# A transformer layer on one core: the merge's elementwise work is taken off the pool engine, and weights are split by whole chunks

## The chip, the cores and the metric

The program runs on one core of a Trainium2 chip. The time is the device time of one execution in microseconds (us). The engines have separate instruction streams and meet at semaphores: PE multiplies matrices (with its weight load, PEld), DVE, ACT and POOL work elementwise, and SP issues most of the loads.

## The reference

One layer for 1024 tokens of width 1024, with 256 context tokens, all in fp32:

```
h   = rmsnorm(x, norm1)*(1+sc1) + sh1                  # in-projection, attention and mLSTM read this
x   = x + g1 * ((sig(g_mla)*attention + sig(g_ml)*mlstm) @ w_out)
h2  = rmsnorm(x, norm2)*(1+sc2) + sh2
aff = softmax(h2 @ w_router)                           # 16 experts
gate, idx = top_k(aff.T, 128)                          # each expert takes its 128 best tokens
y_e = ((silu(xs @ w_gate_e) * (xs @ w_up_e)) @ w_down_e) * gate,   xs = h2[idx_e]
x   = x + g2 * scatter_add(y);   out = rmsnorm(x, final_norm)
```

The result is compared at fp32 accuracy. The kernel splits every operand of a large product into a rounded high part (type fp32r) and the rest as a low part, and adds three products: high by high, high by low, low by high. So each weight has a cast (the high part, on ACT) and a subtraction (the low part) before PE can use it.

## The kernel before, in words

The stages follow one another: norm and in-projection (to about 560 us), the mLSTM and the query projection, attention from about 815 us, the merge from 1258 us, the end of the top-k search from 1402 us, the experts from 1434 us to 2010 us, and the final norm. A scheduler has fixed each engine's order when the program was built; each engine then works in that order, and an instruction that waits holds all behind it.

**Attention** works in 32 groups (8 heads by 4 blocks of 256 queries). For each group PE writes scores `s` for all 1280 keys in five tiles of 128x512. `scores` (L1515 to L1539) takes the running maximum `mx` on DVE (L1529, then four of L1532) and folds it into `mm` (L1536). PE transposes `mm` (L1545, in `peak`), DVE reduces again (L1548), and the maximum goes back as a row that is added to the scores by further products, after which ACT takes the exponent (L1584, `exps`). POOL adds the exponents up (L1590). `low` subtracts on DVE (L1599, tiles `tl`), `finish` (L1632 to L1636) multiplies the group's output by its gate and its denominator (`w`, L1630 and L1635) and adds it to the array `xca` that the out-projection reads (L1636).

**The merge** takes eight tiles of 128 tokens. `half` (L1021) makes high and low parts of the out-projection's weight, eight subtractions of 128x1024 at L1024; those in the table `POOL` go to POOL, the others to DVE. `prep` (L1028) does the same for a tile of `xca` (L1032: tile 0 on DVE, tiles 1 to 7 on POOL). `project` multiplies (L983), adds to the residual (L1086, L1087) and takes the norm's factor `rs` with a Newton iteration on DVE (L1094, L154 to L159). `route` transposes the tile, multiplies by the router's weights and takes the softmax (L1130 to L1134). `store_h` writes the normalized tokens to memory: ACT scales by `rs` (L1139), POOL multiplies by norm2's scale (L1143) and adds its shift (L1147). `largest` finds candidates for each expert's 128 best (MAX8 and MATCH_REPLACE8, L940 and L942, and merges of sorted lists with minimum and maximum, L913 and L914). It runs at tiles 4, 5, 6 and 7, with lists of 64, 16, 16 and 16. `top.last` ends the search with the threshold `thr` (L967).

**The experts** come from one stream of chunks of 1 MB, 12 for each expert: 0 to 3 and 4 to 7 for gate and up (tiles `pa`, `pu`), 8 to 11 for down (`py`). `Weights.load` issues a chunk into one of 16 raw buffers (`raw_l`, `xca`, `ha`, `raw_e`, all lent by other stages), `Weights.split` makes `hi` and `lo` of half a chunk, 128x1024, into one of four pairs of buffers (cast L875 on ACT, subtraction L876 on DVE, on POOL for the first three). `products` asks for the split four halves ahead. `pick(e)` marks on POOL which token stands at which place (L1257, eight operations of 128x128), lets PE sum the marks into indices (`aux`, L1190), and gathers the tokens `xg` with an indirect DMA (L1278). It is called two experts ahead, after chunk 5. `turn_x` transposes gathered tokens on PE (L1287) and splits them (`xh`, L1289, and `xl`, L1290); `turn` does the same for the hidden values (`hd`). At an expert's end DVE scales `py` into `y` (L1353) and POOL adds it to memory (L1354).

Of the kernel before, what the change touches and what calls it, by code (L numbers as in the profile page):

```python
# [23 lines left out]
F32 = mybir.dt.float32  # L24
# [35 lines left out]
N_HAP, N_EARLY, N_MID, N_LATE, N_HI = 2, 3, 4, 7, 4  # L60
# [6 lines left out]
POOL = ((4, 0), (6, 0), (2, 1), (6, 1))  # L67
# [8 lines left out]
def body(tc, A, out, dbg=None, upto=99):  # L76
# [669 lines left out]
    with ExitStack() as s6:  # L746
# [17 lines left out]
        moe(tc, A, out, aff, thr, W, h2_d, acc_d, ident, rstd_dve, dump)  # L764
# [5 lines left out]
class Weights:  # L770
# [19 lines left out]
    def ahead(self):  # L790

        self.wout = [self.outputs(2 * m, self.wide(F32)) for m in range(N_HAP)]
        self.rows = [[self.row(self.narrow(), r, o, 512) for o in (0, 512)] for r in (0, 2)]
# [11 lines left out]
    def load(self, upto):  # L805
        while self.loaded < min(upto, 12 * NE):
# [3 lines left out]
            if j in ONCE:  # L810
                t = self.once[j]
                loads = [self.nc.sync.dma_start(t[c], src[:, c, :]) for c in range(self.begun.pop(j, 0), 2)]
            else:
                b = self.buffer(SEQ.index(j) if j < len(SEQ) else j - 2)
                t = b[:, 0], b[:, 1]
# [3 lines left out]
            if self.after is not None:  # L819
# [4 lines left out]
                if j >= N_RAW + 2 or j in (ONCE[0], 14, 15, 16, 17):  # L824
                    self.after = None
# [32 lines left out]
    def halves(self):  # L858
        return [self.hi.tile([P, D], F32R, name=x, bufs=N_HI) for x in ("hi", "lo")]

    def split(self, upto, engine=None):

        while self.cut < min(upto, 24 * NE):
            j, c = divmod(self.cut, 2)
            self.load((SEQ.index(j) if j < len(SEQ) else j) + 1)
            w = self.raw[j][c]
            if self.cut < 24 * NE - 8:
                hi, lo = self.halves()
            else:
                both = self.buffer(self.cut - 12 * NE + 6, F32R)  # L870
                hi, lo = both[:, 0, :], both[:, 1, :]
            self.parts[self.cut] = hi, lo
            if len(w.shape) == 3:
                hi, lo = [t.rearrange("p (c d) -> p c d", d=256) for t in (hi, lo)]
            self.nc.scalar.copy(hi, w)  # L875
            done = (engine or self.nc.vector).tensor_sub(lo, w, hi)  # L876
# [93 lines left out]
class Merge:  # L970
# [50 lines left out]
    def half(self, k, hf, h, l):  # L1021
        w = self.raw[k][:, :, hf * 512:hf * 512 + 512]
        self.nc.scalar.copy(h, w)
        (self.nc.gpsimd if (k, hf) in POOL else self.nc.vector).tensor_sub(l, w, h)  # L1024
# [3 lines left out]
    def prep(self, i, t):  # L1028
# [3 lines left out]
        (self.nc.vector if i == 0 else self.nc.gpsimd).tensor_sub(ml, self.xca[:, :, c], mh)  # L1032
# [19 lines left out]
    def rest(self, aff, thr, pool):  # L1052
# [7 lines left out]
        g1r, a2 = W.rows  # L1060
        t = W.last(N_FIRST + 1)
        t_buf = t[:, 0, :]
        sh2 = W.row(t[:, 1, :], 1, 0, D)

        def project(i):
# [5 lines left out]
            for hf in order:  # L1071
                o = slice(hf * 512, hf * 512 + 512)
                if (i, hf) not in self.ps:
# [5 lines left out]
                    elif i >= 4:  # L1079
# [29 lines left out]
        def largest(i):  # L1109
            n, part = (64, aff[:, 4:8]) if i == 4 else (16, aff[:, 8 - i:10 - i])  # L1110
# [933 lines left out]
```

## Time and profile before

| what | value |
|---|---|
| median of 3 runs | 2041.03 us (2039.46 to 2044.31) |
| the profiled execution | 2041.3 us, span 2039.5 us, granted clock 0.979 |
| PE busy | 1910.6 us, 94% |
| DVE, ACT, POOL busy | 1462.2, 1048.9, 602.0 us |
| attention to merge to experts | 816, 1258, 1434 us |
| last product | 2010.4 us |

The span runs from the first to the last instruction of the profiled execution; its own time is 1.8 us more. PE's busy share says little on its own, since a few per cent of idle time is all that other engines can give back. So the reading goes by stage: in which stretch PE stands still, and for whom.

### The profile page before, as it was taken

The numbers are of one execution on the slowest core, as the hardware profiler recorded it, in microseconds if no ns is written. First come the engines' busy times: TensorE is split into PE (matmuls) and PEld (weight loads), VectorE is DVE, ScalarE is ACT, GpSimd is POOL, SyncE is SP. The second block draws the span as 40 slices with busy tenths as digits, with TensorE's granted clock in tenths as the row PEclk, the third lists the DMA queues.
The fourth block names the chain that finished last, engine by engine and source line by source line (L and its number), as shares of the span: only waits on it lengthen the run. The fifth ranks groups of instructions, "written<-read, shape, count | busy, mean of one in ns | idle before, by whom it ended". The sixth has DMA issues, their size and how long they took to land. (4 is left out here: it accounts for less than half of the span.)

```text
span 2039.5 us, 28755 instructions
## 1 busy us (share of the span) xinstructions
PE 1910.6 (94%) x10458; PEld 1614.1 (79%) x10458; DVE 1462.2 (72%) x2704; ACT 1048.9 (51%) x1677; POOL 602.0 (30%) x527
## 2 busy tenths in 40 slices
PE   7999999999999999899999998985999999999994
PEld 3898888888877878889998987863778778787873
DVE  6454555112477888687877788578899999999997
ACT  5554421123247676434334434321777777777774
POOL 0000000000043040275434446433453634536310
PEclk9999999999999999999999998997999999999997
DMA  7143376222187060323111111636899999999975
GB/s 302 58 149 100 106 248 220 76 93 89 61 279 248 22 221 1 94 71 117 50 47 50 37 53 58 246 133 224 292 375 380 372 381 369 383 382 364 388 240 187
DMA packets 156301, 385.84 MB, mean 189 GB/s; under 512 B 10224, under 2 KB 94784, under 8 KB 137088
## 3 DMA queue, kind: packets, MB, share of 16 engines
q1 hardware_dynamic: 141104, 329.73, 44.9%
q0 software_dynamic: 12752, 45.90, 7.4%
q10 hardware_dynamic: 2304, 8.39, 1.1%
q8 instruction: 82, 1.34, 0.3%
q14 instruction: 59, 0.48, 0.1%
HBM read 327.04 MB, written 56.93 MB: 188 GB/s over the span
## 5 line engine op out<-in xcount | busy, mean ns | idle before, releaser
L86 PE MATMUL mm<-hT,whi 128*128 128x512 f32 (+1 forms) x1392 | 414.8, 381 | 2.6 <-DVE hT L305 2.3
L86 PEld LDWEIGHTS mm<-hT,whi 128*128 128x128 f32 x1392 | 255.1, 189 | 52.0 <-DVE hT L305 2.4
L86 PE MATMUL mm<-hT,wlo 128*128 128x512 f32 (+1 forms) x696 | 262.9, 378 | 0.3 <-DVE wlo L90 0.3
L876 DVE TENSOR_TENSOR lo<-raw_l,hi 128x1024 fp32r<-128x1024 f32 x156 | 188.1, 1235 | 11.2 <-ACT hi L875 8.2
L1257 POOL TENSOR_SCALAR g<-iota,slot 128x128 bf16<-128x128 f32 x120 | 192.4, 1624 | 0.0
L875 ACT CAST hi<-raw_l 128x1024 fp32r<-128x1024 f32 x156 | 163.3, 1053 | 48.2 <-PE pu L1190 33.8
L1190 PE MATMUL py<-hi,hd 128*128 128x512 f32 x480 | 160.8, 399 | 0.0
L86 PEld LDWEIGHTS mm<-hT,wlo 128*128 128x128 f32 x696 | 131.2, 189 | 24.5 <-DVE wlo L90 0.7
L90 DVE TENSOR_TENSOR wlo<-wraw,whi 128x1024 fp32r<-128x1024 f32 x38 | 46.5, 1224 | 142.8 <-ACT whi L89 142.8
L1590 POOL TENSOR_TENSOR es<-es,e 128x512 f32<-128x512 f32 x96 | 126.4, 1317 | 7.0
L1590 POOL TENSOR_TENSOR es<-e 128x512 f32<-128x512 f32 x32 | 41.8, 1305 | 272.4 <-ACT e L1584 272.4
L876 DVE TENSOR_TENSOR lo<-xca,hi 128x1024 fp32r<-128x1024 f32 x96 | 115.3, 1231 | 6.6 <-ACT hi L875 4.8
L1584 ACT ACTIVATE e<-s 128x512 f32<-128x512 f32 x160 | 94.5, 612 | 47.1 <-PE s L1432 47.1
L1354 POOL DMA_INDIRECT acc_d<-y,idx x15 | 34.9, 2328 | 270.4 <-DVE y L1353 270.4
L875 ACT CAST hi<-xca 128x1024 fp32r<-128x1024 f32 x96 | 100.1, 1051 | 27.6 <-PE pu L1190 20.0
L89 ACT CAST whi<-wraw 128x1024 fp32r<-128x1024 f32 x38 | 40.0, 1051 | 128.8 <-PE mm L86 120.4
L1190 PEld LDWEIGHTS py<-hi,hd 128*128 128x128 f32 x480 | 89.7, 188 | 17.9
L1190 PE MATMUL pa<-hi,xh 128*128 128x512 f32 x256 | 102.4, 400 | 0.3 <-ACT xh L1289 0.3
L1190 PE MATMUL pa<-lo,xh 128*128 128x512 f32 x256 | 99.9, 390 | 1.1 <-DVE lo L876 1.1
L1190 PE MATMUL pu<-lo,xh 128*128 128x512 f32 x256 | 99.8, 390 | 0.0
L1190 PE MATMUL pu<-hi,xl 128*128 128x512 f32 x256 | 99.8, 390 | 0.0
L1190 PE MATMUL pa<-hi,xl 128*128 128x512 f32 x256 | 99.7, 390 | 0.0
(509 smaller groups left out, 5088.2 us busy)
## 6 DMA issues: line engine op xcount, KB each, us to landing
raw_l<-in_wgu SPq DMA_DIRECT2D x54, 1024.0 KB
xca<-in_wgu SPq DMA_DIRECT2D x33, 1024.0 KB
raw_l<-in_wd SPq DMA_DIRECT2D x28, 1024.0 KB
raw_e<-in_wgu SPq DMA_DIRECT2D x24, 1024.0 KB
wraw<-in_win SPq DMA_DIRECT2D x38, 512.0 KB
wt<-in_wmod_b SPq DMA_DIRECT2D x32, 512.0 KB
ha<-in_wgu SPq DMA_DIRECT2D x16, 1024.0 KB
xca<-in_wd SPq DMA_DIRECT2D x15, 1024.0 KB
```

Source lines behind the costliest of these rows:

```text
L86: return TE.matmul(o, l, r, start=start, stop=stop, skip_group_check=True)
L89: S.copy(hi, raw)
L90: V.tensor_sub(lo, raw, hi)
L875: self.nc.scalar.copy(hi, w)
L876: done = (engine or self.nc.vector).tensor_sub(lo, w, hi)
L1190: return TE.matmul(o, l, r, start=start, stop=stop, skip_group_check=True)
L1257: G.tensor_scalar(oh[:, o, :], iota, slot[:, o, e:e + 1], None, op0=ALU.is_equal)
L1354: G.indirect_dma_start(out=acc_d, out_offset=bass.IndirectOffsetOnAxis(ap=idx[e][:, :1], axis=0), in_=y, in_offset=None, compute_op=ALU.add)
L1584: S.activation(E[p], ps, AF.Exp)
L1590: G.tensor_add(s, E[0] if p == 1 else s, E[p])
```

## The change

- **Attention.** `finish` no longer adds `w` to `xca`. The addition is kept in a table `ADD` and issued one group later, in `peak2`, behind the last `tl` there. `w` has three buffers for two.
- **Merge.** All subtractions of `half` and `prep` go to DVE. `store_h` only scales by `rs` on ACT and stores; norm2's scale and shift are no longer loaded as rows. `largest` runs at tiles 4, 6 and 7, with lists of 64, 32 and 16.
- **Gathered tokens.** `turn_x` applies norm2's scale and shift after the transposition, where they are a number for each partition: eight operations of 128x128 an expert, on ACT (half of them on DVE for expert 0), from PSUM into a buffer of 128x512 that is then split.
- **Splits.** A cast and a subtraction take a whole chunk, 128x2048, into one of three pairs of whole buffers; `products` asks three chunks ahead. The first is on DVE too. Raw buffers go from 16 to 14, and the loads ahead of the experts from (1, 3, 6, 6, 7, 7, 9, 9) by tile to (1, 3, 4, 4, 5, 5, 7, 7).
- **Picking.** The marks (`mark`) are asked for after chunk 3, and the sums and the gather (`pick`) after chunk 9.
- **Tail.** The last loads and stores of the tokens use contiguous rows of 1024.

```diff
 class Weights / constants
-N_HAP, N_EARLY, N_MID, N_LATE, N_HI = 2, 3, 4, 7, 4
+N_HAP, N_EARLY, N_MID, N_LATE, N_HI = 2, 1, 4, 7, 3
-POOL = ((4, 0), (6, 0), (2, 1), (6, 1))
     def halves(self):
-        return [self.hi.tile([P, D], F32R, name=x, bufs=N_HI) for x in ("hi", "lo")]
+        return [self.hi.tile([P, 2, D], F32R, name=x, bufs=N_HI) for x in ("hi", "lo")]
     def split(self, upto, engine=None):
...
-            self.nc.scalar.copy(hi, w)
-            done = (engine or self.nc.vector).tensor_sub(lo, w, hi)
+            for h, l, w in views:
+                self.nc.scalar.copy(h, w)
+                done = (engine or self.nc.vector).tensor_sub(l, w, h)
 half, prep
-        (self.nc.gpsimd if (k, hf) in POOL else self.nc.vector).tensor_sub(l, w, h)
+        self.nc.vector.tensor_sub(l, w, h)
-        (self.nc.vector if i == 0 else self.nc.gpsimd).tensor_sub(ml, self.xca[:, :, c], mh)
+        self.nc.vector.tensor_sub(ml, self.xca[:, :, c], mh)
 project, largest
-                    elif i >= 4:
+                    elif i in (4, 6, 7):
-            n, part = (64, aff[:, 4:8]) if i == 4 else (16, aff[:, 8 - i:10 - i])
+            n, part = {4: (64, aff[:, 4:8]), 6: (32, aff[:, 2:4]), 7: (16, aff[:, 1:3])}[i]
 store_h
-            if i < 7:
-                S.activation(u, x, AF.Copy, scale=rs)
-            for hf in range(2):
...
-                    G.tensor_mul(u[:, o], u[:, o], a2[hf])
...
-            added = G.tensor_add(u, u, sh2)
+            scaled = S.activation(u, x, AF.Copy, scale=rs)
             nc.scalar.dma_start(self.h2_d[i * P:(i + 1) * P], u)
 rest
-            W.load((1, 3, 6, 6, 7, 7, 9, 9)[i])
+            W.load((1, 3, 4, 4, 5, 5, 7, 7)[i])
-        W.split(N_HI - 1, G)
+        W.split(1)
 moe
         with tc.issue_after(counted.ins):
-            done = W.split(N_HI)
+            done = W.split(2)
         def turn_x(e, q):
...
+            for c in range(4):
+                k, o = 4 * q + c, slice(c * P, (c + 1) * P)
+                sc, sh = bcols[:, 16 + k:17 + k], bcols[:, 8 + k:9 + k]
+                if e == 0 and c % 2:
+                    V.tensor_scalar(t[:, o], tr[:, o], sc, sh, op0=ALU.mult, op1=ALU.add)
+                else:
+                    S.activation(t[:, o], tr[:, o], AF.Identity, scale=sc, bias=sh)
+            hi, lo = [x[:, 4 * q:4 * q + 4, :].rearrange("p a b -> p (a b)") for x in xsT[e]]
+            split(hi, lo, t)
         def products(j, ps, l, start, stop):
-                W.split(2 * j + c + N_HI)
+            W.split(j + N_HI)
+            W.load(N_RAW + j + N_HI + 2 - sum(o < j + N_HI for o in ONCE))
...
-                    if hf == 1 and q == 1 and e + 2 < NE:
-                        pick(e + 2)
+                    if hf == 0 and q == 3 and e + 2 < NE:
+                        mark(e + 2)
...
+                    if q == 1 and e + 2 < NE:
+                        pick(e + 2)
                     if q in (1, 2):
                         turn_x(e + 1, q - 1)
 the tail
-                    nc.sync.dma_start(x[:, a], acc_d[i * P:(i + 1) * P].rearrange("p (c d) -> p c d", d=256))
+                    nc.sync.dma_start(x[:, a], acc_d[i * P:(i + 1) * P])
 attention: peak2, finish
                 for p in PARTS[2:]:
                     low(g - 1, p)
+                if g > 1:
+                    add(g - 2)
...
-            V.tensor_add(xc[h][:, c], xc[h][:, c], w)
+            ADD[g] = xc[h][:, c], w
+            if g >= NG - 2:
+                add(g)
```

Three places of the engines' orders show what moves. In the rows stand the line, the operation, out<-in by the program's names, and the size of the output; line numbers after the change are those of the changed file. The first is DVE in the middle of attention, from one group's gate to the next; before, the addition (L1636) stands ahead of the four maxima (L1532):

```order
L1630 TENSOR_TENSOR w<-s,g_9475 128x256
L1635 TENSOR_TENSOR w<-pv,w 128x256
L1529 TENSOR_REDUCE mx<-s 128x256
L1636 TENSOR_TENSOR xca<-xca,w 128x256
L1532 TENSOR_TENSOR mx<-mx,s 128x512 x4
L1536 TENSOR_TENSOR mm<-mx 128x256
L1599 TENSOR_TENSOR tl<-e,th 128x512
```

With the change:

```order
L1650 TENSOR_TENSOR w<-s,g_9470 128x256
L1655 TENSOR_TENSOR w<-pv,w 128x256
L1547 TENSOR_REDUCE mx<-s 128x256
L1550 TENSOR_TENSOR mx<-mx,s 128x512 x4
L1554 TENSOR_TENSOR mm<-mx 128x256
L1619 TENSOR_TENSOR tl<-e,th 128x512
L1566 TENSOR_REDUCE mq<-sm 128x2
L1619 TENSOR_TENSOR tl<-e,th 128x512
L1579 TENSOR_TENSOR qm_9851<-sm,qm_9851 32x256
L1619 TENSOR_TENSOR tl<-e,th 128x512
L1663 TENSOR_TENSOR xca<-xca,w 128x256
L1454 TENSOR_TENSOR kl_9865<-s,kh_9864 128x512
```

The addition (L1663) now stands behind the third `tl`, and nothing is between the first maximum and the four that follow.

The second is DVE at the end of the top-k search, from the threshold to the first indices. Before, one half-chunk subtraction (L876) stands between the counting (L1235) and the places `slot` (L1250):

```order
L967 TENSOR_REDUCE thr<-bt_13580 16x1
L1211 CAST cst<-g_13609 128x256
L1231 TENSOR_TENSOR mk<-aff,tr 128x8x16
L1232 TENSOR_TENSOR mk<-aff,tr 128x8x16
L1235 TENSOR_REDUCE above<-mk 128x16
L876 TENSOR_TENSOR lo<-ha,hi 128x1024
L1248 SCALAR_TENSOR_TENSOR g_13644<-tr,mk 128x256
L1250 SCALAR_TENSOR_TENSOR slot<-g_13644 128x128
```

With the change:

```order
L971 TENSOR_REDUCE thr<-bt_13501 16x1
L1208 CAST cst<-g_13529 128x256
L1228 TENSOR_TENSOR mk<-aff,tr 128x8x16
L1229 TENSOR_TENSOR mk<-aff,tr 128x8x16
L1232 TENSOR_REDUCE above<-mk 128x16
L880 TENSOR_TENSOR lo<-ha,hi 128x2048
L1245 SCALAR_TENSOR_TENSOR g_13564<-tr,mk 128x256
L880 TENSOR_TENSOR lo<-raw_e,hi 128x2048
L1247 SCALAR_TENSOR_TENSOR slot<-g_13564 128x128
```

Two whole-chunk subtractions stand there now; a third (chunk 0) stands further ahead, between the last MAX8 and the minima of the last merge.

The third is DVE from an expert's last hidden half (`hd`) to its output (`y`). Before, half-chunk subtractions alternate with the small work:

```order
L1290 TENSOR_TENSOR hd<-tr,hd 128x512
L876 TENSOR_TENSOR lo<-ha,hi 128x1024 x2
L1290 TENSOR_TENSOR xl<-tr,xh 128x512
L876 TENSOR_TENSOR lo<-raw_e,hi 128x1024 x2
L1290 TENSOR_TENSOR xl<-tr,xh 128x512
L876 TENSOR_TENSOR lo<-raw_e,hi 128x1024
L1353 SCALAR_TENSOR_TENSOR y<-py_15958,gt,g2row 128x512
```

With the change:

```order
L880 TENSOR_TENSOR lo<-raw_l_15281,hi 128x2048
L880 TENSOR_TENSOR lo<-raw_l_15299,hi 128x2048
L1290 TENSOR_TENSOR hd<-tr,hd 128x512
L1270 COPY ax<-tr 128x5
L1273 SCALAR_TENSOR_TENSOR idx<-ax 128x1
L1274 TENSOR_TENSOR gt<-ax 128x1
L880 TENSOR_TENSOR lo<-raw_l_15322,hi 128x2048
L1275 TENSOR_TENSOR gt<-gt,ax 128x1
L1184 TENSOR_TENSOR xl<-g_15684,xh 128x512
L880 TENSOR_TENSOR lo<-raw_l_15347,hi 128x2048
L1371 SCALAR_TENSOR_TENSOR y<-py_15613,gt,g2row 128x512
```

The last hidden half stands behind the subtractions of chunks 10 and 11, the indices of the pick behind it, and the second half of the gathered tokens behind `y`.

More of the change, by code (lines that the diff above doesn't have):

```diff
@@ L763, in body @@
             return
-        moe(tc, A, out, aff, thr, W, h2_d, acc_d, ident, rstd_dve, dump)
+        moe(tc, A, out, aff, thr, W, h2_d, acc_d, ident, bcols, rstd_dve, dump)
     hap.__exit__(None, None, None)
@@ L792, in ahead @@
         self.wout = [self.outputs(2 * m, self.wide(F32)) for m in range(N_HAP)]
-        self.rows = [[self.row(self.narrow(), r, o, 512) for o in (0, 512)] for r in (0, 2)]
+        self.rows = [self.row(self.narrow(), 0, o, 512) for o in (0, 512)]
     def wide_hi(self, dtype):
@@ L813, in load @@
             else:
-                b = self.buffer(SEQ.index(j) if j < len(SEQ) else j - 2)
-                t = b[:, 0], b[:, 1]
+                t = b = self.buffer(SEQ.index(j) if j < len(SEQ) else j - 2)
                 if len(b.shape) == 4:
@@ L1059, in rest @@
         nc.sync.dma_start(wr, A["wrouter"])
[L1060 to L1063, printed above, removed]
+        g1r = W.rows
+        t_buf = W.last(N_FIRST + 1)[:, 0, :]
         def project(i):
@@ L1182, in rest, with moe, split @@
         self.st.close()
-def moe(tc, A, out, aff, thr, W, h2_d, acc_d, ident, rstd, dump):
+def moe(tc, A, out, aff, thr, W, h2_d, acc_d, ident, bcols, rstd, dump):
     nc = tc.nc
     V, S, G, TE = nc.vector, nc.scalar, nc.gpsimd, nc.tensor
+    def split(hi, lo, raw):
+        S.copy(hi, raw)
+        V.tensor_sub(lo, raw, hi)
     def mm(o, l, r, start, stop):
@@ L1250, in moe, with mark @@
         V.scalar_tensor_tensor(slot, taken[:, :, 0, :], -1.0, taken[:, :, 1, :], op0=ALU.add, op1=ALU.add)
-        gat, idx, xg, xsT, hid = {}, {}, {}, {}, {}
-        def pick(e):
-            oh = W.narrow().bitcast(BF16).rearrange("p (a b) -> p a b", b=P)
+        gat, idx, xg, xsT, marks = {}, {}, {}, {}, {}
+        def mark(e):
+            oh = marks[e] = W.narrow().bitcast(BF16).rearrange("p (a b) -> p a b", b=P)
             for o in range(8):
@@ L1260, in pick @@
                                 slot[:, o:o + 4, e:e + 1].to_broadcast([P, 4, P]), op=ALU.is_equal)
+        def pick(e):
+            oh = marks.pop(e)
             ap = ps7.tile([P, 512], F32, name="tr", bufs=2)
@@ L1317, in act @@
             return h
+        mark(0)
         picked, got, W.after = pick(0)
@@ L1323, in moe @@
         with tc.issue_after(W.after.ins):
+            mark(1)
             pick(1)
@@ L1628, in weigh2 @@
             tr = along(*W[g])
-            w = W[g] = p5.tile([P, 256], F32, name="w", bufs=2)
+            w = W[g] = p5.tile([P, 256], F32, name="w", bufs=3)
             V.tensor_mul(w, tr, G1[g // 2][:, cols(g)])
```

64 lines of the change are left out of this document (36 added, 28 removed).

## The prediction

> **What bounds the kernel now.** I read the busy times by stage first, then PE's waits in each stage, then the timelines of the engines waited for. The window view has for each stretch (start to end, length) the busy us and instructions of PE, PEld, DVE, ACT and POOL, then granted clock, DMA share and GB/s:
>
> ```profile
> 816.00:1225.00 409.00, 388.21 (x2892) 363.00 (x2892) 309.45 (x545) 161.79 (x329) 193.89 (x169) 0.99 0.20 65
> 1258.00:1326.00 68.00, 63.34 (x313) 51.23 (x312) 46.20 (x70) 23.32 (x44) 41.55 (x19) 0.92 0.59 210
> 1326.00:1402.00 76.00, 64.13 (x326) 50.05 (x325) 61.52 (x280) 20.06 (x41) 25.72 (x15) 0.96 0.52 183
> 1402.00:1434.00 32.00, 9.77 (x50) 6.95 (x49) 24.00 (x76) 3.29 (x7) 18.21 (x22) 0.57 0.47 179
> 1470.00:1978.00 508.00, 493.17 (x2351) 404.37 (x2350) 473.81 (x502) 392.56 (x422) 219.66 (x144) 1.00 1.00 367
> ```
>
> PE stands still for 21 us in attention, 17 in the merge, 22 at the end of the search and 15 in the experts. These idle times are the purse; no edit takes products away. I take each part of the change against the stretch that it lies in. The sum is made against the profiled execution, 2041.3 us, which is 0.3 us above the median of the runs.
>
> **Attention.** PE's wait in the stretch 860 to 1225, then the addition over the whole program, then one group's DVE and PE rows:
>
> ```profile
> PE sm L1545 <- DVE mm L1536: 13.8, 25, 1.0
> ...
> L1636 DVE TENSOR_TENSOR xca<-xca,w x32: 419/1398/2603, 855.4 to 1268.2; 128x256 f32<-128x256 f32 x32
> ...
> 1018.73 3.05 DVE L1532 TENSOR_TENSOR mx<-mx,s 128x512 f32<-128x512 f32 x4
> 1021.82 0.61 DVE L1536 TENSOR_TENSOR mm<-mx 128x256 f32<-128x256 f32 x1
> ...
> 1020.22 0.28 PE L1432 MATMUL s<-qp,kpe 128*128 128x256 f32 x1
> 1021.66 0.28 PE L1432 MATMUL pv<-th,vl 128*128 128x256 f32 x1
> 1022.49 0.44 PE L1545 MATMUL sm<-ident,mm 128*128 128x128 f32 x2 [0.55 <-DVE mm L1536]
> ```
>
> The addition takes 0.42 us alone, but 1.40 at the median, and it stands ahead of the four maxima that PE's transposition needs. Without it they start 1.4 us earlier, and another limit takes over: the last score is written at 1020.22 + 0.28 = 1020.50, its maximum takes 0.76 (3.05 for four) and the fold 0.61, so `mm` is there at about 1021.87 for 1022.43. PE is free at about 1021.8. So about 0.45 of each 0.55 us goes: 25 waits give 13.8 x 0.45/0.55 = 11.3, and the three groups before 860 about 1 more. I take **-12**, between -8 (a quarter of it lost to the addition where it lands) and -14 (all of it). The addition now stands ahead of `kl`, `ri` and the next gate. DVE has holes of about 0.5 us there, and POOL's sums are done by then, so at 0.42 it is hidden; beside POOL it would cost up to 1 us in some groups, which is the -8.
>
> **The start of the merge.** PE's first products of the merge, the weight's subtractions on DVE, and the same subtraction where POOL is not in the way:
>
> ```profile
> 1262.76 0.80 PE L983 MATMUL mm<-wl,x 128*128 128x512 f32 x1 [2.81 <-DVE wl L1024]
> 1266.60 0.69 PE L1555 MATMUL mm<-ident,ri 128*128 128x128 f32 x2 [1.34 <-DVE ri L1624]
> 1270.07 0.63 PE L983 MATMUL mm<-wl,x 128*128 128x512 f32 x1
> 1270.49 1.05 PE L983 MATMUL mm<-wh,x 128*128 128x512 f32 x2
> 1272.52 0.39 PE L983 MATMUL mm<-wl,x 128*128 128x512 f32 x1
> 1272.75 0.62 PE L983 MATMUL mm<-wh,x 128*128 128x512 f32 x2
> ...
> L1024 DVE TENSOR_TENSOR wl<-ha,wh 128x1024 fp32r<-128x1024 f32 x2 | 6.7, 3386 | 0.0
> ...
> L876 DVE TENSOR_TENSOR lo<-raw_l,hi 128x1024 fp32r<-128x1024 f32 x156 | 188.1, 1235 | 11.2 <-ACT hi L875 8.2
> ```
>
> A subtraction of this size takes 1.24 us on a free DVE and 3.39 here, where POOL subtracts too. Each is held by 2.1 us, so two on the path return up to 4.2, bounded by the two waits, 2.81 + 1.34 = 4.15. Behind the wait products also start only every 0.42 us (1270.07 to 1270.49) for 0.23 later (1272.52 to 1272.75). From 1262.8 to 1271.8 that is about 17 products, 3.3 us. On the other side four subtractions come to DVE from POOL, 4 x 1.24 = 5 us, of which I put 1.5 in front of products that need them. The sum is -4.15 - 3.3 + 1.5 = **-6**; bounds -8 (nothing in front) and -3 (all 5 in front).
>
> The clock gate in the Trainium skill (TensorE: Matmul & The Clock Gate, Part 1) halves PE's clock after an idle window of about 3.4 us and restores it after a busy one of the same length. By that rule the slow stretch would cost 3.4/2 = 1.7 us, and this part would come to -4.4. The trace shows the slow rate for 9 us, with a second wait in it, so the measurement decides.
>
> **The middle of the merge.** PE's waits from 1258 to 1402, then two groups of DVE instructions (busy us, mean ns of one) in that stretch, and a run of products:
>
> ```profile
> PE tr L1121 <- issue: 6.3, 2, 3.4
> PE so L954 <- DVE bt L914: 2.2, 1, 2.2
> PE so L946 <- DVE rv L154: 1.6, 2, 1.4
> PE tr L1121 <- DVE x L1087: 1.0, 1, 1.0
> ...
> L1087 DVE TENSOR_TENSOR x<-x,raw_l 128x512 f32<-128x512 f32 x8 | 9.4, 1174 | 1.2 <-DMA x<-in_x 1.1
> L1134 DVE TENSOR_SCALAR aff<-aff,mx 128x16 f32<-128x16 f32 x7 | 7.0, 995 | 0.1
> ...
> 1372.29 2.77 PE L983 MATMUL mm<-raw_l,raw_l 128*128 128x512 f32 x6
> ```
>
> L1134 works on 16 numbers a partition and takes 995 ns, where its neighbours of that size take 0.2: it is held while POOL works. L1087 takes 1.17 for 0.68 (the row of 512 columns below). These two groups alone return 7 x 0.8 + 8 x 0.5 = 9.6 us of DVE. PE's waits here are 11.1 us, and the six products in 2.77 us are a slow stretch behind the 3.4 us wait (0.46 each for 0.23); two such stretches add some 3, so about 14 can be won. Part of it stays: the search's waits (L954, L946) depend on sorts that remain at tiles 4, 6 and 7. Against it stand seven `prep` subtractions that come to DVE, 7 x 1.24 = 8.7 us, and for it the search at tile 5 that goes; the last one, below, runs from 1411.66 to 1421.53, 9.9 us with 2.0 of holding, so about 8. These two cancel. I take 14 - 4 = **-10**, between -14 and -4 (the `prep`s on DVE stand ahead of the residual's additions and hold the transpositions by 1.2 us at five or more tiles).
>
> **The end of the search.** From the last tile to the first product of an expert everything is one chain on DVE, with short steps on PE. Its rows, with POOL's work that holds them:
>
> ```profile
> 1401.52 2.40 DVE L914 TENSOR_TENSOR sd<-se 16x64 f32<-16x64 f32 x1
> 1403.85 2.30 DVE L159 SCALAR_TENSOR_TENSOR rs<-rt,ry 128x1 f32<-128x1 f32 x1
> 1408.55 2.39 DVE L1134 TENSOR_SCALAR aff<-aff,mx 128x16 f32<-128x16 f32 x1
> 1411.66 0.21 DVE L940 MAX8 sc<-so 64x8 f32<-64x64 f32 x1
> 1416.82 2.20 DVE L913 TENSOR_TENSOR se<-sd 16x64 f32<-16x64 f32 x1
> 1421.53 0.28 DVE L924 TENSOR_TENSOR bt<-sd,best 16x128 f32<-16x128 f32 x1
> ...
> 1401.50 4.64 POOL L876 TENSOR_TENSOR lo<-ha,hi 128x1024 fp32r<-128x1024 f32 x2 [11.54 <-ACT hi L875]
> ```
>
> Four small operations take 9.3 us for about 0.8, so POOL's leaving returns 8.5, and the two scalings of tile 7 (L1146, 0.7 each) 1.4. Into this chain come three subtractions of a whole chunk. From 1.24 for 1024 columns and 0.68 for 512 (below), 0.56 for each 512, such a one takes about 2.3 on DVE. One stands in the last merge, two behind the counting in place of one of 1.2: 3 x 2.3 - 1.2 = +5.7. The scale and shift of the gathered tokens add about +1.2, four short operations each on ACT and DVE. Together -8.5 - 1.4 + 5.7 + 1.2 = **-3**. If the subtractions fall where DVE waits for PE anyway it is -7; if POOL's remaining casts hold DVE as before, +1.
>
> **The experts.** PE's waits from 1470 to 1990, the outputs' first and last start, eight marks beside busy DVE and beside an idle one, and a subtraction of 512 columns and two casts of 1024:
>
> ```profile
> PE tr L1190 <- POOL g L1257: 13.6, 12, 1.1
> ...
> L1353 DVE SCALAR_TENSOR_TENSOR y<-py,gt,g2row x30: 740/744/747, 1470.4 to 1978.0; 128x512 f32<-128x512 f32 x30
> ...
> 1510.23 13.86 POOL L1257 TENSOR_SCALAR g<-iota,slot 128x128 bf16<-128x128 f32 x8
> 1428.98 4.70 POOL L1257 TENSOR_SCALAR g<-iota,slot 128x128 bf16<-128x128 f32 x8
> ...
> 1521.73 0.68 DVE L1290 TENSOR_TENSOR hd<-tr,hd 128x512 fp32r<-128x512 f32 x1
> ...
> 1407.43 1.98 ACT L875 CAST hi<-ha 128x1024 fp32r<-128x1024 f32 x2
> ```
>
> An expert takes (1978.0 - 0.7 - 1470.4)/14 = 36.2 us. PE waits 1.1 in most of them for the last mark. Moved to the end of chunk 9, `pick` comes some 12 us later, and that wait goes: -13.6. Another takes its place. Chunk 8's end frees the buffer for chunk 11: cast 2.0, subtraction 2.3, and behind both the last `hd`, 0.7, ready 5.1 us after chunk 8 with the handovers. PE reaches the next transpositions, which need its PSUM buffer, after four transpositions, 12 products, the eight short sums and four products: 0.4 + 16 x 0.23 + 0.2 = 4.3. So it waits about 0.8 at 14 handovers: +11. For the last two experts the order puts a subtraction ahead of or behind `y` where PE needs it, +0.8 each. Together -13.6 + 11 + 1.6 = **-1**. Bounds: -8 (half of the handovers hidden, and nothing at the last two) and +8 (a whole 2.3 instead of 0.8 at some six handovers). PE's waits in this stretch name no load, with 16 buffers and 367 GB/s; with 14 an expert's 12 chunks still fit ahead of it, so I cost that at nothing, and two chunks' time, 6 us, is what the stock ahead of PE shrinks by. In the tail the same chain stays, **-0.5** for larger descriptors.
>
> **The sum** is -12 - 6 - 10 - 3 - 1 - 0.5 = -32.5: 2041.3 - 32.5 = **2009 us**.
>
> **Rivals.** *DVE takes POOL's place in the merge.* For it: DVE is busy 61.5 of 76 us before anything is added, and it gets 11 subtractions, 13.6 us. Against it: much of that is time held, 9.6 us in the two groups alone. If a third is won, the start, the middle and the end give -6 for -19: 2041.3 - 12 - 6 - 1.5 = 2022. Chance 0.16. *The scores bound attention.* If the maxima, which follow the scores one by one, leave only 0.1 of the 0.55 to win, attention gives -3 for -12: 2018. Against it stands 1.4 us of addition in front of them. Chance 0.08. *The change finds no idle time to return*, because each wait is replaced by one as long: 2041. Chance 0.03. *Marks too late: slower.* Eight marks take 4.70 us alone and 13.86 beside half-chunk subtractions, 1.73 each, 0.5 more than a subtraction. Beside 2.3 they take 8 x 2.8 = 22. They are asked for after chunk 3, six chunks of 3.03 = 18 us before the sums. If they start only then, PE waits 4 us at 14 experts, +56 and the 0.8 on top: 2041.3 - 31.5 + 56 + 11 = 2077. It decides from 18 us for eight marks. Against it: in POOL's order they stand right behind the gather before, so they can start some 12 chunks ahead. Chance 0.07.
>
> The Trainium skill (SBUF — State Buffer, Who interferes with whom) states that a DVE instruction with two SBUF inputs and a reading GpSimd one exclude each other for a whole instruction. That is the pricing of this last rival; the trace agrees at 1401.52, where 0.2 became 2.40 beside a POOL operation of 2.3.
>
> **How the numbers follow.** My forecast has 0.66. Faster by over 0.2% (4 us, about what a measurement of this kernel can tell) are it and the first two rivals, 0.90; within it 0.03; slower 0.07. The bounds of the terms, taken together, reach from about 1990 to above 2030, and hardly all lie at one end: the range 1995 to 2029 takes in the first two rivals and leaves out the slow one.
>
> **What would show it.** Right: the wait of `sm` for `mm` under 4 us; `wl` and L1134 at 1.2 and 0.2 us; no slow stretch of products in the merge; 1402 to 1434 shorter by about 3; outputs `y` 36.1 apart, with PE waiting at the gathered tokens for `hd`, not for marks. Wrong: marks on PE's waits, a merge as long as before with DVE full, or experts more than 36.6 apart.

## The result and the profile after

The changed kernel takes 2005.79 us (median of 4 runs, 2002.72 to 2007.51) against 2041.2 us: a ratio of 0.9823, with a 95% interval of 0.9806 to 0.9841. That is 35.4 us less; forecast were 32, to 2009. The total was right, most of its terms were not, and the experiments below say why.

I cut both traces at the same instructions: the first transposition of `mm` in attention, the first product of the merge, the softmax of tiles 0 and 7 (its last step), the first product of expert 0, and PE's last product. The lengths between them, in us:

| stretch | before | after | difference | forecast |
|---|---|---|---|---|
| start to attention | 832.4 | 834.5 | +2.1 | 0 |
| attention | 426.2 | 419.8 | -6.4 | -12 |
| merge, to the softmax of tile 0 | 38.5 | 29.4 | -9.1 | -6 |
| merge, to the softmax of tile 7 | 111.5 | 93.4 | -18.1 | -14.3 |
| end of the search, to the first product | 25.4 | 28.5 | +3.0 | +1.3 |
| experts | 576.8 | 573.0 | -3.8 | -1 |
| tail | 28.7 | 26.4 | -2.3 | -0.5 |
| span | 2039.5 | 2004.9 | -34.6 | -32.5 |

(Forecast: two of the four held operations that the prediction counted at the end, L914 and L159, 4.3 us, lie ahead of tile 7's softmax and are counted in the merge here.) The first row lies in stages that the change does not touch and moves between 832.4 and 835.5 in the profiles below. Where a kernel leaves the other stretches alone, attention and the start of the merge repeat to about 1 us either way, the rest to a few tenths. So the runs below are read by stretches, and by medians for the sum.

The window view of the changed kernel, for attention, the merge, the end of the search and the experts (columns as in the prediction):

```profile
816.00:1221.00 405.00, 388.32 (x2895) 360.70 (x2894) 296.67 (x555) 163.29 (x335) 195.43 (x169) 0.99 0.21 65
1254.00:1377.00 123.00, 119.83 (x636) 96.49 (x634) 80.71 (x326) 43.66 (x86) 1.09 (x3) 1.00 0.59 209
1377.00:1405.50 28.50, 9.04 (x53) 6.62 (x53) 20.53 (x79) 6.99 (x9) 10.43 (x19) 0.59 0.64 252
1444.70:1942.80 498.10, 490.26 (x2342) 400.14 (x2342) 456.16 (x333) 399.42 (x364) 248.47 (x142) 1.00 1.03 378
```

The merge is now all but full on PE: 119.8 of 123.0 us at a clock of 1.00, where it was 127.6 busy of 150.0 at 0.93. DVE works 80.7 us in it where it was 113.6 busy, although it got 11 subtractions more and only one search less. In attention 16.7 us of idle time stay. Here are two of PE's waits before, from 860 to 1225, and then its waits in the changed kernel from 800 to 1225, from 1376 to 1408 and from 1443 to 1945. A single wait of 6.6 us ahead of the first maximum (6.0 before) is left out:

```profile
PE sm L1555 <- DVE mq L1548: 0.9, 3, 0.3
PE s L1621 <- DVE kl L1436: 0.2, 1, 0.2
...
PE sm L1573 <- DVE mq L1566: 3.6, 19, 0.5
PE sm L1563 <- DVE mm L1554: 3.4, 6, 1.2
PE s L1641 <- DVE kl L1454: 1.8, 8, 0.2
...
PE tr L1187 <- DVE g L1256: 5.1, 2, 4.7
PE tr L1187 <- DVE g L1305: 1.5, 1, 1.5
...
PE tr L1299 <- DVE hd L1290: 6.1, 12, 0.5
PE pa L1187 <- DVE lo L880: 1.7, 1, 1.7
```

From 860 to 1225 the wait for `mm` fell from 13.8 to 3.2 us, but those for `mq`, the second maximum, and for `kl` grew, from 0.9 to 3.1 and from 0.2 to 1.8. The experts wait 0.5 us for the last hidden half instead of 1.1 for a mark. The operations that POOL held before are at their free length (groups of DVE, and the whole-chunk subtractions and outputs):

```profile
L1028 DVE TENSOR_TENSOR wl<-ha,wh 128x1024 fp32r<-128x1024 f32 x2 | 2.3, 1212 | 0.0
L1136 DVE TENSOR_SCALAR aff<-aff,mx 128x16 f32<-128x16 f32 x8 | 1.8, 227 | 0.1
L880 DVE TENSOR_TENSOR lo<-raw_l,hi 128x2048 fp32r<-128x2048 f32 x92 | 210.8, 2298 | 21.9 <-ACT hi L879 19.6
...
L1371 DVE SCALAR_TENSOR_TENSOR y<-py,gt,g2row x30: 733/742/746, 1444.7 to 1943.4; 128x512 f32<-128x512 f32 x30
```

`wl` takes 1.21 for 3.39 us, the softmax's last step 0.23 for 1.0. Outputs are 35.6 us apart for 36.3 (here and below the mean of the first twelve intervals, ahead of the last experts).

### The profile page after: what moved, and what is told of

Read it like the earlier page. It is cut to its first block, busy times and chain, and to the rows that moved or that the text cites. A ratio compares the mean times of both kernels' runs of the same rounds, so it can differ in the third digit from the quotient of the medians.

```text
span 2004.9 us, 28234 instructions
## 1 busy us (share of the span) xinstructions
PE 1906.5 (95%) x10454; PEld 1607.3 (80%) x10454; DVE 1397.4 (70%) x2492; ACT 1060.5 (53%) x1611; POOL 554.3 (28%) x491
## 5 line engine op out<-in xcount | busy, mean ns | idle before, releaser
L880 DVE TENSOR_TENSOR lo<-raw_l,hi 128x2048 fp32r<-128x2048 f32 x92 | 210.8, 2298 | 21.9 <-ACT hi L879 19.6
L1254 POOL TENSOR_SCALAR g<-iota,slot 128x128 bf16<-128x128 f32 x120 | 206.5, 1733 | 0.0
L879 ACT CAST hi<-raw_l 128x2048 fp32r<-128x2048 f32 x92 | 176.1, 1916 | 34.6 <-PE pu L1187 25.8
L1187 PE MATMUL py<-hi,hd 128*128 128x512 f32 x496 | 168.3, 401 | 0.0
L880 DVE TENSOR_TENSOR lo<-xca,hi 128x2048 fp32r<-128x2048 f32 x54 | 123.6, 2297 | 17.5 <-ACT hi L879 16.5
L879 ACT CAST hi<-xca 128x2048 fp32r<-128x2048 f32 x54 | 102.9, 1907 | 25.5 <-PE pu L1187 19.7
L1550 DVE TENSOR_TENSOR mx<-mx,s 128x512 f32<-128x512 f32 x128 | 87.8, 686 | 27.2 <-PE s L1450 24.6
L1278 POOL DMA_INDIRECT xg<-h_d,idx x16 | 35.8, 2235 | 255.9 <-PE tr L1299 238.2
L1578 ACT CAST qm<-sm 64x256 fp32r<-64x256 f32 x32 | 11.8, 367 | 167.8 <-PE sm L1573 167.8
```

The source lines that it names most:

```text
L880: done = (engine or self.nc.vector).tensor_sub(l, w, h)
L1187: return TE.matmul(o, l, r, start=start, stop=stop, skip_group_check=True)
L1254: G.tensor_scalar(oh[:, o, :], iota, slot[:, o, e:e + 1], None, op0=ALU.is_equal)
L1278: got = G.indirect_dma_start(out=xg[e], out_offset=None, in_=h2_d, in_offset=bass.IndirectOffsetOnAxis(ap=idx[e][:, :1], axis=0))
L1550: V.tensor_max(new if p > 1 else new.rearrange("p (a b) -> p a b", a=2), old, ps if p > 1 else ps.rearrange("p (a b) -> p a b", a=2))
```

## The experiments

**The addition alone.** The kernel before with only this (and a third buffer for `w`):

```diff
                 for p in PARTS[2:]:
                     low(g - 1, p)
+                if g > 1:
+                    add(g - 2)
...
-            V.tensor_add(xc[h][:, c], xc[h][:, c], w)
+            ADD[g] = xc[h][:, c], w
+            if g >= NG - 2:
+                add(g)
```

> The kernel before with the put-off addition alone. Theory of the prediction (the addition stands in front of the maximum that PE waits for; PE's wait of 13.8 us goes by four fifths): -12, about 2029 us. Theory after the two traces (the stretch from the first to the last transposition of mm became 7.4 us shorter, because a new wait for mq takes back 0.3 us a group): -7, about 2034 us, all of it between 830 and 1250, and a wait of PE for mq of about 3.5 us. Rival (the scores and their maxima bound the groups, and the shorter stretch has another cause): no change, 2041 us.

2033.28 us, ratio 0.9959 (0.9945 to 0.9973): -9.0 by medians, with the interval from -11 to -6. In the profile attention is 6.8 us shorter (426.2 to 419.3) and every later stretch as before. PE's waits from 820 to 1240:

```profile
PE sm L1545 <- DVE mm L1536: 3.8, 7, 1.2
PE sm L1555 <- DVE mq L1548: 3.7, 20, 0.5
```

The addition is worth about 7, not 12, and the longer wait for `mq` comes with it.

**The addition back in its place,** in the changed kernel (with two buffers for `w`):

```diff
-                if g > 1:
-                    add(g - 2)
...
-            if g >= NG - 2:
-                add(g)
+            add(g)
```

> The changed kernel with the addition back in its old place (two buffers for w). If the addition's place is what attention gained by, 2006 + 7 = 2013 us, with PE's wait for mm back at about 14 us and the merge and the experts as long as in the changed kernel. Rival (the merge's start gains by additions that are no longer in front of it): 2 to 3 us more is lost at the merge's first products, 2016 us. Rival (no effect of the addition): 2006 us.

2011.03 us, 0.9858 (0.9842 to 0.9874). Attention is 425.8 us long again, 6.0 more than in the changed kernel, and the wait is back:

```profile
PE sm L1563 <- DVE mm L1554: 14.3, 26, 1.0
```

The merge's start is 29.7 for 29.4, so the rival that it gains by the missing additions falls. From both sides the addition gives 6 to 7 us.

**The second maximum first.** Why only 7? The changed kernel's DVE and POOL in one group:

```profile
1020.40 0.42 DVE L1554 TENSOR_TENSOR mm<-mx 128x256 f32<-128x256 f32 x1
1020.75 1.22 DVE L1619 TENSOR_TENSOR tl<-e,th 128x512 fp32r<-128x512 f32 x1
1021.89 0.41 DVE L1566 TENSOR_REDUCE mq<-sm 128x2 f32<-128x256 f32 x1
...
1020.48 0.94 POOL L1612 TENSOR_TENSOR eh<-es 128x256 f32<-128x256 f32 x1
```

With `mm` earlier, the first `tl` meets POOL's last sum and takes 1.22 for 0.68; the reduction to `mq` stands behind it. The edit, on top of the changed kernel, issues that `tl` behind the reduction:

```diff
-            halved = V.tensor_max(MX[g], mx[:, :256], mx[:, 256:])
-            with tc.issue_after(halved.ins):
-                low(g - 1, 0)
+            V.tensor_max(MX[g], mx[:, :256], mx[:, 256:])
...
             with tc.issue_after(found.ins):
+                low(g - 1, 0)
                 low(g - 1, PARTS[1])
```

> The changed kernel with one thing added in attention: on DVE the second maximum (mq) goes ahead of the first low part, which in the changed kernel stands in front of it and is held to 1.22 us by POOL. Theory (mq is what PE waits for now, and the stretch from the transposition of mm to that of mq is 0.33 us a group longer than before): 25 to 30 groups by 0.33 = -8 to -10, 1997 us, less if the low part is then late. Rival (the low part that moves back is waited for by PE instead): no gain, 2006 us.

1998.62 us, 0.9796 (0.9780 to 0.9813). Attention is 414.5 us, 5.3 less than in the changed kernel, all else the same. The same place in this run:

```profile
1019.21 0.42 DVE L1554 TENSOR_TENSOR mm<-mx 128x256 f32<-128x256 f32 x1
1020.16 0.42 DVE L1564 TENSOR_REDUCE mq<-sm 128x2 f32<-128x256 f32 x1 [0.53 <-PE sm L1561]
1020.51 1.28 DVE L1618 TENSOR_TENSOR tl<-e,th 128x512 fp32r<-128x512 f32 x2
```

`mq` starts 0.95 us behind `mm` for 1.49, and two `tl` together take 1.28, since POOL is done by then. Both edits in attention together give 426.2 - 414.5 = 11.7 us, nearly the 12 that the prediction gave the first alone. The expectation of 8 to 10 was too high.

**The low parts alone.** The kernel before with `half` and `prep` on DVE; POOL keeps norm2's scale and shift:

```diff
-        (self.nc.gpsimd if (k, hf) in POOL else self.nc.vector).tensor_sub(l, w, h)
+        self.nc.vector.tensor_sub(l, w, h)
-        (self.nc.vector if i == 0 else self.nc.gpsimd).tensor_sub(ml, ...)
+        self.nc.vector.tensor_sub(ml, ...)
```

> The kernel before with all low parts of the merge on DVE, and nothing else; POOL keeps norm2's scale and shift and the first splits. Theory (whoever is on POOL holds DVE; at the merge's start that is the weight's subtractions, from tile 2 on the scale and shift): from the first product to the softmax of tile 0 about 8 us shorter (38.5 us before, 29.4 in the changed kernel), the rest of the merge only 3 us: 2041 - 11 = 2030 us. Rival (DVE takes POOL's place as the bound): the start gains 4 at most, the middle loses up to 5, and the time stays at 2040 us.

2034.35 us, 0.9963 (0.9951 to 0.9976). To tile 0's softmax the merge takes 29.4 us for 38.5, the whole gain of the change there. From tile 0 to tile 7 it takes 117.1 for 111.5: 5.6 lost, as the rival had it. Of these 2.2 come back in the next stretch, 23.2 us for 25.4, since tile 7's last step is no longer held. At the tiles before it that step is held as before, and PE waits for it (groups of DVE, then PE's waits, both in the merge):

```profile
L1134 DVE TENSOR_SCALAR aff<-aff,mx 128x16 f32<-128x16 f32 x8 | 8.1, 1010 | 0.1
...
PE so L933 <- DVE aff L1134: 11.0, 2, 8.6
```

**The scale and shift alone.** The kernel before with the new `turn_x` and `store_h`; low parts, sorts, picks and splits as they were:

```diff
-            if i < 7:
-                S.activation(u, x, AF.Copy, scale=rs)
-            for hf in range(2):
...
-            added = G.tensor_add(u, u, sh2)
+            scaled = S.activation(u, x, AF.Copy, scale=rs)
```

> The kernel before with norm2's scale and shift applied to the gathered tokens, and nothing else; POOL keeps low parts, and picks and splits stay as they were. Theory: the merge's start stays as it was, the middle gains about 8 us (22 us of POOL work that held DVE goes), the end of the search 2, and the experts lose little since the eight small operations on ACT are hidden: 2041 - 9 = 2032 us. Rival (the added operations stand in front of the split of the gathered tokens, and PE waits for them at each expert): experts 1 us longer each, and the sum is 2046 us.

2065.05 us, 1.010 (1.008 to 1.012): slower. The merge from tile 0 to 7 takes 99.0 us for 111.5, so it gains 12.5 there; `wl` is still held and L1134 is free (groups of DVE):

```profile
L1024 DVE TENSOR_TENSOR wl<-ha,wh 128x1024 fp32r<-128x1024 f32 x2 | 6.7, 3400 | 0.0
L1134 DVE TENSOR_SCALAR aff<-aff,mx 128x16 f32<-128x16 f32 x8 | 1.8, 226 | 0.1
```

But the experts take 632.7 us for 576.8, 40.2 between outputs. The profiled execution is the longest of five (2059.25 to 2082.15), so these figures are above the typical ones; by medians the run loses 23 us. The direction of the rival was right and its place wrong: PE does not wait for the scaled tokens. Its waits from 1457 to 2053, and the scatter of `y` that stands ahead of the marks on POOL (shortest, median, longest ns):

```profile
PE tr L1185 <- POOL g L1252: 35.2, 50, 1.8
PE pa L1185 <- DVE lo L876: 8.1, 15, 0.5
...
L1363 POOL DMA_INDIRECT acc_d<-y,idx x15: 2167/2345/10299, 1461.6 to 2022.8; - x15
```

It waits for marks. They stand behind the scatter, and the scatter needs both halves of `y`. Here the second half starts 3.5 us behind the first (1460.61 and 1457.08), with `xl` and a subtraction between them; in the kernel before the two follow one another (1.40 us for both, at 1506.74). In six of the scatters POOL's instruction takes 10.3 us for 2.3, and those experts are the longest. What makes it 10.3 in some and not in others I have not found; one scatter of the half-chunk run below takes 10.9.

**The marks and the pick back.** The changed kernel with both after chunk 5:

```diff
-                    if hf == 0 and q == 3 and e + 2 < NE:
-                        mark(e + 2)
+                    if hf == 1 and q == 1 and e + 2 < NE:
+                        mark(e + 2)
+                        pick(e + 2)
...
-                    if q == 1 and e + 2 < NE:
-                        pick(e + 2)
```

> The changed kernel with marks and pick asked for after chunk 5 again, as before. Eight marks take 15.1 us beside whole-chunk subtractions in the changed kernel, and stand behind the scatter of y. Theory (the early marks are what keeps the experts short; scale and shift alone, with the old place, made each expert 38 to 43 us): outputs 37 us or more apart, 2 us an expert more with PE's wait on the last mark, 2006 + 14 x 2 = 2034 us or more. Rival (the place matters only by the 1.1 us that PE waited before): outputs 36.2 apart, 2006 + 14 x 0.6 = 2014 us. Rival (the whole-chunk splits alone are what helps): 2006 us.

2044.77 us, 1.0015 (1.0005 to 1.0024). The stretches up to the first product are those of the changed kernel, and the experts take 611.9 us for 573.0, 38.6 between outputs: in the changed kernel this one place is worth as much as the whole change. In the kernel before the same place made PE wait 13.6 us in all. PE's waits from 1443 to 1980 and POOL in one expert:

```profile
PE tr L1187 <- POOL g L1254: 26.0, 36, 1.5
...
1561.30 3.39 POOL L1371 DMA_INDIRECT acc_d<-y,idx  x1 [19.15 <-PE pu L1187]
1564.17 13.90 POOL L1254 TENSOR_SCALAR g<-iota,slot 128x128 bf16<-128x128 f32 x8
```

The row of the scatter names PE, but the second half of `y` had ended only 0.3 us ahead of it, at 1561.01. The order is a loop: `y`, scatter, eight marks of 13.9 us, sums on PE, the rest of the expert, the next `y`. By this order whatever makes `y` later on DVE lengthens every expert; the run before this one, where it came later, fits. In the changed kernel the marks stand ahead of the scatter, right behind the gather:

```profile
1512.52 15.13 POOL L1254 TENSOR_SCALAR g<-iota,slot 128x128 bf16<-128x128 f32 x8
1527.82 1.61 POOL L1372 DMA_INDIRECT acc_d<-y,idx  x1 [0.17 <-DVE g L1330]
```

They take longer, 15.1 us, and PE's waits above name none of them.

**Half-chunk instructions,** in the changed kernel with its whole buffers:

```diff
-                views = [(hi, lo, raw)]
+                views = [(hi[:, c], lo[:, c], raw[:, c]) for c in range(2)]
```

> The changed kernel with every cast and subtraction issued as two halves of 128x1024 into the same three whole buffers. DVE works 24 x 1.23 = 29.5 us an expert for 12 x 2.30 = 27.6, ACT 25.2 for 22.9. Theory (an expert's length is set by the order of marks and hidden values, with DVE at nine tenths): outputs 35.6 to 36.1 apart, the end of the search unchanged, 2006 to 2013 us. Rival (the longer instructions are what made experts 0.8 us shorter): 36.4 apart, 2017 us. Rival (long instructions in a queue hurt): 0.5 us shorter each, 1999 us.

2004.29 us, 0.9820 (0.9803 to 0.9836), not to be told from the changed kernel by the times. The edit leaves 54 of the subtractions whole, those whose raw buffer is `xca`. In the profile outputs are 35.3 us apart for 35.6, and the experts 2.2 us shorter. PE's waits from 1443 to 1945:

```profile
PE pa L1187 <- DVE lo L880: 4.2, 9, 0.9
PE tr L1299 <- DVE hd L1290: 2.0, 4, 0.5
```

The longer instructions are not what made the experts shorter; PE waits less for `hd` without them and more for `lo`.

**The search at tile 5 back:**

```diff
-                    elif i in (4, 6, 7):
+                    elif i >= 4:
-            n, part = {4: (64, aff[:, 4:8]), 6: (32, aff[:, 2:4]), 7: (16, aff[:, 1:3])}[i]
+            n, part = (64, aff[:, 4:8]) if i == 4 else (16, aff[:, 8 - i:10 - i])
```

> The changed kernel with the candidate search at tile 5 again (four searches as before, lists of 64, 16, 16, 16). The prediction set the search's 8 us of DVE against the seven added subtractions and called it even. Theory after the runs so far (low parts alone and scale and shift alone make the merge 3.6 and 15 us shorter, the change 27): the search on the path, the stretch from the softmax of tile 4 to that of tile 5 grows from 13.7 to about 20 us, and the time is 2006 + 8 = 2014 us. Rival (it hides under PE's products now that DVE is free of POOL): 2007 us.

2007.49 us, 0.9835 (0.9819 to 0.9851); in the profile 1.4 us more. Tile 5's softmax is 4.4 us later, tile 7's 3.0, and the end of the search, with a shorter list to merge, gives 1.4 back. The rival was right: most of a search hides, once POOL no longer holds DVE.

**The tail back to rows of 256:**

```diff
-                x = W.buffer(12 * NE + 2 + m)
+                x = W.middle(m)
...
-                    nc.sync.dma_start(x[:, a], acc_d[i * P:(i + 1) * P])
+                    nc.sync.dma_start(x[:, a], acc_d[i * P:(i + 1) * P].rearrange("p (c d) -> p c d", d=256))
```

> The changed kernel with the tail's buffers, loads and stores in rows of 256 again, as before. From PE's last product to the end it took 28.7 us before and 26.4 in the changed kernel. Theory (the larger contiguous rows are what gains 2.4): 2006 + 2.4 = 2008 us, with 28.7 at the tail. Rival (the gain comes from elsewhere, such as which buffers are free): 26.4 at the tail, 2006 us. The prediction's value was 0.5.

2022.44 us, 0.9917 (0.9900 to 0.9933). In the changed kernel these buffers hold weights of the last expert; the run reads the tokens over them, so it computes something else and its last expert is 12 us longer. It does not answer the question. The tail's 2.3 us are left as the trace has them: from PE's last product to the last scaling 17.4 us for 18.5, and from there to the end 9.0 for 10.3.

**The subtractions behind the gather.** Two whole-chunk subtractions stand between the counting and the indices of expert 0 in the changed kernel (DVE):

```profile
1389.68 2.28 DVE L880 TENSOR_TENSOR lo<-ha,hi 128x2048 fp32r<-128x2048 f32 x1
1392.21 2.28 DVE L880 TENSOR_TENSOR lo<-raw_e,hi 128x2048 fp32r<-128x2048 f32 x1
```

The edit issues them behind the indices:

```diff
-        with tc.issue_after(counted.ins):
-            done = W.split(2)
...
         picked, got, W.after = pick(0)
+        with tc.issue_after(picked.ins):
+            W.split(3)
```

> The changed kernel with the subtractions of chunks 1 and 2 behind the indices of the first expert, while the gather is under way, and not ahead of them. Theory: in the changed kernel they stand in the chain from the threshold to the gather for 2 x 2.28 us, and DVE then is idle for 6.3 us; moved, the gather comes 4.5 us earlier and so does the first product: 2006 - 4.5 = 2001.5 us. Rival (the chain then waits for something else, the store of tile 7's tokens or a cast): less than 2 us, 2004 us. Rival (the subtractions now hold the scaling of the gathered tokens or the first products): no gain, 2006 us.

2005.45 us, 0.9823 (0.9807 to 0.9839). The gather starts 3.1 us earlier behind the threshold, the first product only 0.8. In this run POOL, DVE and PE show

```profile
1393.71 2.58 POOL L1276 DMA_INDIRECT xg<-h_d,idx  x1 [14.36 <-DVE gt L1273]
...
1393.06 2.28 DVE L880 TENSOR_TENSOR lo<-ha,hi 128x2048 fp32r<-128x2048 f32 x1
...
1399.90 1.94 PE L1297 MATMUL tr<-ident,xg 128*128 128x128 f32 x8 [3.45 <-DMA xg<-h_d,idx]
```

The gather's instruction takes 2.58 us, where it took 1.07 in the changed kernel, and the tokens come 6.2 us after its start. Whether the subtraction does that is the next run.

**The same, behind the gather's instruction.** The two subtractions also wait for the small POOL operation behind the gather:

```diff
+        for n in (2, 3):
+            tc.add_manual_dep(W.split(n).ins, W.after.ins.name, ...)
```

> As the run with the subtractions of chunks 1 and 2 behind the gather, but they now also wait until POOL has written the gather's descriptors. In that run the gather's instruction took 2.58 us for 1.07 and its data came 6.2 us after its start for 4.6, beside a subtraction of 2.28. Theory (the subtraction holds POOL): the instruction is back at 1.07, the tokens 1.5 us earlier, the first product 2 us earlier than in that run: about 2003.5 us. Rival (the data's way is what was longer, and DVE has no part in it): as in that run, 2005 us.

2005.15 us, 0.9831 (0.9815 to 0.9848). Its POOL and PE rows:

```profile
1394.18 1.06 POOL L1276 DMA_INDIRECT xg<-h_d,idx  x1 [14.05 <-DVE gt L1273]
1395.32 13.99 POOL L1252 TENSOR_SCALAR g<-iota,slot 128x128 bf16<-128x128 f32 x16
...
1398.83 1.06 PE L1297 MATMUL tr<-ident,xg 128*128 128x128 f32 x8 [0.98 <-DMA xg<-h_d,idx]
1402.23 0.19 PE L1187 MATMUL tr<-aux,g 128*128 128x5 bf16 x1 [0.39 <-POOL g L1252]
```

The instruction is back at 1.06 and the tokens come 4.6 us after its start: the subtraction held POOL. But the held thing is now the marks behind it, 13.99 us for 16 (9.7 in the changed kernel), and PE stands at expert 1's sums, which are ahead of its first product. The first product is 1.4 us earlier against the softmax of tile 7 than in the changed kernel.

**All of it, with expert 1's sums later.** The changed kernel with the second maximum first, the two subtractions behind the gather's instruction, and now the pick of expert 1 behind two chunks of products:

```diff
-            pick(1)
...
+                    if e == 0 and hf == 0 and q == 1:
+                        with tc.issue_after(done.ins):
+                            pick(1)
```

> The changed kernel with the second maximum first, the subtractions of chunks 1 and 2 behind the gather's descriptors, and one thing more: the sums for expert 1 behind the first two chunks of products, since in the run before PE waited at them for marks, 4 x 0.39 us, that the subtractions had made late. Theory (the three gains add: 5.5 in attention, 3.5 at the first product): 2006 - 9 = 1997 us, with the first product 3.5 us earlier against the merge's end than in the changed kernel. Rival (the first expert then waits for its fourth chunk, whose cast needs the first chunk's buffer, and only the 1.4 of the run before is left): 1999 us. Rival (expert 1's tokens are now late): 2000 us or more, with PE's wait at the second expert's transpositions.

1996.58 us, 0.9786 (0.9771 to 0.9802): faster than both kernels, 44.7 us below the one before by medians. From tile 7 to the first product it takes 25.4 us for 28.5, and attention 414.3. Against the run with the second maximum alone, 1998.62, the rest is not told apart by the times. Part of the 3.1 us is given back in the first expert, 40.3 us to its output for 39.3, and 1.6 in the merge, where the order of the search came out another way. PE's first products in this run:

```profile
1397.99 0.80 PE L1187 MATMUL pa<-hi,xh 128*128 128x512 f32 x1 [2.19 <-ACT xh L1183]
1398.59 0.63 PE L1187 MATMUL pa<-lo,xh 128*128 128x512 f32 x1
...
1402.85 0.63 PE L1187 MATMUL pu<-hi,xl 128*128 128x512 f32 x1
1403.28 0.48 PE L1187 MATMUL pa<-hi,xh 128*128 128x512 f32 x1
1403.60 0.39 PE L1187 MATMUL pa<-lo,xh 128*128 128x512 f32 x1
1403.83 0.40 PE L1187 MATMUL pu<-hi,xh 128*128 128x512 f32 x1
```

Products start every 0.43 us up to 1403.3 and every 0.23 from then on: twelve at the slow rate, 2.4 us, behind the pause.

## Why the prediction was right, and where it was not

The total of -32.5 met -35.4, inside the range, but by errors of both signs; that they nearly cancel is luck.

- **Attention: mis-sized, -12 for -6.7.** The wait for `mm` went nearly as forecast, by 10.6 us for 11.3, and the addition takes 0.42 us in its new place at the median, as said (1.50 at most). The step that failed is "So about 0.45 of each 0.55 us goes", which counts as gained what `mm` frees and follows the path no further. Once `mm` ends 0.7 us earlier (5.0 us behind the last multiplication of `w` for 5.7, medians), the first low part runs into POOL's sums and is held, and `mq` stands behind it: from the transposition of `mm` to that of `mq` it takes 1.33 us for 1.14 on average, 6 us over the 32 groups. With `mq` first it takes 1.10, and that run gives 5.3 us more. A smaller part is `kl`, ahead of which the addition now stands: PE waits 1.6 us more for it, and no run has that alone. The rival that the scores bound attention was half right: DVE waits 0.27 us for its scores at each of the four maxima in the group above, but that is not what cost the gain.
- **The start of the merge: -9.1 for -6.** The mechanism was right, as the low parts alone give all of it. The 1.5 us set in front of products were not lost; PE waits 0.6 us for `wl`, and the slow stretch is gone.
- **The middle: -18.1 for -14.3.** The seven `prep` subtractions, 8.7 us, were set even against the dropped search, 8. The search does not give that, and the sums below leave no such cost for the subtractions, though no run has them alone. The whole merge gains 3.6 us by the low parts alone and 14.9 by the scale and shift alone, 18.5 in sum; with all four searches the changed kernel gains 24.2. The 5.7 beyond the sum fit POOL's first splits (in the kernel before they hold two small DVE operations there, 4.3 us), which were still on POOL in both runs and held three small DVE operations by 2.1 us each in one and one in the other, ahead of tile 7's softmax; no run has them alone. So the parts add as far as the runs show, and the subtractions on DVE seem to be paid for by DVE's own freed time. The dropped search brings 3.0 in the merge and costs 1.4 of it at the end.
- **The end of the search: +3.0 for +1.3.** Three subtractions of 2.28 us came into the chain as forecast (2.3). From the threshold to the first product it became 5.3 us longer: 3.4 for the subtractions (two of 2.28 for one of 1.21) and the rest in the scaling of the tokens, which the prediction had at 1.2 and which takes 1.8 on either engine, with PE waiting 1.5.
- **The experts: -3.8 for -1, from terms of other sizes.** The place of the handover was right: PE waits for `hd` at the gathered tokens. It waits 0.5, not 0.8, 13 times. Each steady expert is 0.7 to 0.8 shorter. The first is 2.9 longer (39.3 for 36.4 from its first product), nine of its products at the slow rate; and the two waits for `lo` at the last experts, which were to cost 0.8 each, are 1.7 each. From the last `y` to PE's last product it takes 35.7 us for 33.4. The whole-chunk instructions, to which the change gives most of its lines, do nothing for the time here, as far as the run that halves most of them tells.
- **The tail: -2.3 for -0.5,** not settled.
- **The rivals.** DVE taking POOL's place shows in the run with the low parts alone, and only there. The slow one, marks too late, was excluded for the right reason, their place in POOL's order: put back together with the pick, they cost 39 us, where the prediction had 67 with the handover. Its price for eight marks was too high (22 us; 15.1 beside whole chunks).

## What to carry to other kernels

Where two engines hold each other, look at which work of the one stands beside the path of the other: norm2's scale and shift off POOL gave 14.9 us, the larger part of the merge's gain, and the low parts off it 3.6. By itself the first made the kernel slower, as PE then waited for marks in the experts. After removing a stall, read what the next instruction on that engine now runs beside, at its new time. And a piece of work that looks like bookkeeping, here when the marks and the pick are asked for, can be worth as much as everything else, since it closes a loop from one expert's output to the next.

## What the runs showed of the hardware

An indirect gather's instruction on POOL took 2.58 us beside a DVE subtraction with two inputs from SBUF, and 1.06 when that subtraction waited for it; the tokens came 6.2 and 4.6 us after its start. The experts show the same. In the changed kernel each of the 14 gathers there starts while a whole-chunk subtraction runs and ends 0.8 to 0.9 us behind that one's end, so 13 of them take 2.4 to 2.5 us:

```profile
1509.26 2.29 DVE L880 TENSOR_TENSOR lo<-xca,hi 128x2048 fp32r<-128x2048 f32 x1
...
1509.97 2.47 POOL L1278 DMA_INDIRECT xg<-h_d,idx  x1 [16.16 <-PE tr L1299]
```

In the kernel before, 11 of 14 take 1.05 us, and there the subtraction starts 0.4 to 0.5 us behind the gather. So a subtraction that is already running holds the gather's instruction, and one that starts behind it does not. The Trainium skill (SBUF — State Buffer, Who interferes with whom) says that `tensor_tensor` was not seen to stall such DMAs; here the measurement differs. The instruction also reads its indices `idx`, and no run tells whether that reading is what waits.

PE's slow rate came behind pauses of 2.8 us (merge, before) and of 2.2 us that followed a shorter one (first product, last run), and lasted for 9 us, with a second pause in it, and for 5.3 us without one. In the 3.7 us up to the end of the first pause PE did one product, and in the 4.4 us up to the end of the second only eight transpositions. In the first expert of the changed kernel four products start at the full rate, and then all from 1406.69 to 1410.08 start about every 0.43 us, 3.4 us long. The Trainium skill (TensorE: Matmul & The Clock Gate, Part 1) has about 3.4 us for both; the last stretch agrees, the unbroken 5.3 us do not, and the pauses do not decide it.
